# Expert groups of two and of three: another order within each layer

## The chip, the cores and the metric

The kernel runs on one core of a Trainium2 chip. The core has TensorE (PE in the profile) for matrix products, VectorE (DVE), ScalarE (ACT) and GpSimd (POOL) for the rest, and SyncE (SP), which here only issues transfers. Sixteen DMA engines carry the transfers of all queues. The metric is the device time of one execution in microseconds (us). [...]

## The reference, cut to what matters

The model is a trunk of two residual layers over 256 tokens of width 1024, all in float32, with a final norm. Each layer has attention, and then a mixture of sixteen experts, of which each token uses two:

```
aff = sigmoid(xf @ router_w)                  # 256 x 16
# the best of four groups of experts, in it the best two: expert (256 x 2), weight w (256 x 2)
for each expert e, for the tokens that chose it:
    h = silu(x @ w_gate[e]) * (x @ w_up[e])   # 1024 -> 512
    y = h @ w_down[e]                         # 512 -> 1024
x = x + gate_f * (sum over the two experts of w * y)
```

Each expert has three matrices of 2 MB, 6 MB in all; a layer's sixteen experts are 96 MB. Which expert gets how many tokens is known only when the router has run.

## The kernel before

The kernel never reads fewer than all experts. It sorts fourteen of the sixteen experts of a layer by their number of tokens (`places`, line 1357) and gives each a place with room for 96, 64 or 32 tokens: `GROUPS` (line 31) lists seven groups of places as (place, blocks of 32), each group 128 places wide, and `RANKS` (line 33) says which rank of the sorted experts goes to which place. The first group, places 14 and 15, is not sorted and holds the fixed experts 14 and 15, so its weights can be loaded before the router has run. Group 1 has two experts (96 and 32 places), groups 2 and 4 have three (64, 32, 32), groups 3, 5 and 6 have two (64 and 64). Tokens beyond an expert's room are done in overflow rounds.

A group's work (`Group`, line 1211) is: `hidden` loads gate and up and multiplies (16 steps over k, in each step one product per block of columns), `turn` transposes, `rows` loads down and multiplies (8 steps), and `late` adds the result to X. The loop at line 1464 runs `hidden` of group i, then `rows` of group i-1, then the gather of tokens for two later groups in every second turn.

Loads. Every matrix comes in two loads of 1 MB (`load_experts`, line 1161). They go into fifteen buffers of 1 MB, ten called slot and five called room. `left` (line 150) writes the cycle in which they are handed out: in layer 0 two rooms, five slots, three rooms, five slots; in layer 1 three rooms, six slots, two rooms, four slots. The cycle begins with four loads for the conditioning, then the eight of group 0's gate and up; the loads that need the router's result begin with the thirteenth. A load waits until its buffer has been given back by its last reader; of buffers of one kind the one given back first is taken first. SyncE issues nearly all loads, in the order of the program.

Line 1466 is the place that matters below. When the loop comes to group 3, the down of group 2 is loaded, the last sums are added, and `rest` (line 1445) reserves six buffers for overflow rounds and puts seven nested rounds behind a branch on their number. TensorE, ScalarE, VectorE and SyncE take this branch; with this input no round is needed. Group 3's own twelve loads are issued by GpSimd (`self.after`), which does not take the branch; SyncE goes on with group 4 behind it.

```
def left(n, then, more):
    order[:] = ["wx"] * n + ["w"] * then + ["wx"] * more + ["w"] * (RING - then)
...
def rest():
    space = [slot(4, 512) for _ in range(6)]
...
if i == 3:
    before.load_down()
    flush()
    rest()
```

In layer 1 the last group ends the kernel (`finish`, line 1283): its down comes in three pieces of 512, 256 and 256 columns (`load_down`, line 1251), and each is multiplied, weighted and added in turn, then the final norm is applied and stored.

Of the kernel before, what the change touches and what calls it, by code (L numbers as in the profile page):

```python
# [27 lines left out]
RING, EXTRA = 10, 5  # L28


GROUPS = [[(14, 2), (15, 2)], [(0, 3), (1, 1)], [(2, 2), (3, 1), (4, 1)], [(5, 2), (6, 2)], [(7, 2), (8, 1), (9, 1)],
          [(10, 2), (11, 2)], [(12, 2), (13, 2)]]
RANKS = 0, 9, 1, 10, 11, 2, 3, 4, 12, 13, 5, 6, 7, 8
SORTED = len(RANKS)
BLOCK = 32


def shape_constants():
# [40 lines left out]
    iota = np.tile(1000 + np.arange(96, dtype=f)[None], (P, 1))  # L79
    ranks = np.tile(np.array(RANKS, f)[None], (P, 1))  # L80
    places = sorted(x for g in GROUPS for x in g)
    size = np.tile(np.array([BLOCK * n for _, n in places], f)[None], (P, 1))

    owner = np.concatenate([np.repeat(np.eye(len(g), dtype=f), [BLOCK * n for _, n in g], axis=0) for g in GROUPS], axis=1)
    rank = np.tile((4 - np.arange(4)).astype(f)[None], (P, 1))
# [22 lines left out]
def trunk(ctx, tc, ins, out):  # L108
# [30 lines left out]
    def slot(n_k, n):  # L139

        tag = order.pop(0)
        order.append(tag)
        t = room() if tag == "wx" else ring.tile([P, 2048], F32, tag="w", name="slot")
        return t[:, :n_k * n].rearrange("p (k f) -> p k f", k=n_k)

    def room():

        return rooms.tile([P, 2048], F32, tag="wx", name="room")
# [818 lines left out]
    def moe(cp, wk, layer, norm, end):  # L967
# [119 lines left out]
        def blocks(group):  # L1087


            ns = [n for _, n in group]  # L1090
            if ns == [2, 2]:
                return [(1, slice(64, 128)), (0, slice(0, 64))]
            at = [a for a, n in enumerate(ns) for _ in range(n)]
            return [(at[j], slice(BLOCK * j, BLOCK * j + BLOCK)) for j in reversed(range(4))]
# [66 lines left out]
        def load_experts(nm, experts, k, tiles=None, queue=sp, fine=False):  # L1161

            out = [[] for _ in experts]
            for h in range(2):
                for i, e in enumerate(experts):
                    t = tiles.pop(0) if tiles else slot(4, 512)
                    v = ins[nm][layer][bass.ds(e, 1)].rearrange("o (p k) f -> p (o k) f", k=k)
                    n = k // 2
                    t = t.rearrange("p a b -> p (a b)").rearrange("p (k f) -> p k f", k=n)
                    if not (fine and h):  # L1170
                        queue.dma_start(t, v[:, n * h:n * h + n, :])
                    out[i].append((t, n))
            for k0 in range(0, n if fine else 0, 2):
                for x, e in zip(out, experts):
                    v = ins[nm][layer][bass.ds(e, 1)].rearrange("o (p k) f -> p (o k) f", k=k)
                    queue.dma_start(x[1][0][:, k0:k0 + 2, :], v[:, n + k0:n + k0 + 2, :])
            return [Rows(x) for x in out]
# [11 lines left out]
        def pick_tile():  # L1189
            return wk.tile([P, 2, 256], F32R, tag="pick", name="pick")  # L1190

        def picked(groups, pos):

            o = pick_tile()
            places, at = [x for g in groups for x in GROUPS[g]], 0
            while places:
# [14 lines left out]
        class Group:  # L1211


            def __init__(self, i, o, XG, c0):
                self.first, self.last = i == 0, (layer, i) == (1, len(GROUPS) - 1)
                self.after = i == 3
                self.o, self.XG, self.c0 = o, XG, c0
                self.p0, self.n = GROUPS[i][0][0], len(GROUPS[i])
                self.parts = blocks(GROUPS[i])
                first = sum(len(g) for g in GROUPS[:i])  # L1220
                self.owner = const("owner")[:, first:first + self.n]
                es = list(range(self.p0, self.p0 + self.n))
                if i:
                    es = [load_value(ex_p[:, e:e + 1], [(ET.SP, ET.Pool)[self.after]], NE - 1) for e in es]
                self.es = es
                self.Wd = None
# [24 lines left out]
            def load_down(self):  # L1251
                if self.Wd is not None:
                    return
                if not self.last:
                    self.Wd = load_experts("moe_w_down", self.es, 4, queue=(sp, pool)[self.after])
                    return

                src = [ins["moe_w_down"][layer][bass.ds(e, 1)].rearrange("o (p k) f -> p (o k) f", k=4) for e in self.es]
                self.Wd = []
                for sl, step in zip(end.pieces, (2, 4, 2)):  # L1260
                    n = sl.stop - sl.start
                    if n == 512:
                        tiles = [slot(4, n) for _ in range(2)]
                    else:
                        tile_ = slot(8, n)
                        tiles = [tile_[:, 0:4], tile_[:, 4:8]]
                    for k in range(0, 4, step):
                        for t, v in zip(tiles, src):
                            sp.dma_start(t[:, k:k + step], v[:, k:k + step, sl])
                    self.Wd.append(tiles)  # L1270
# [507 lines left out]
```

## Time and profile before

| | |
|---|---|
| median of 3 runs | 868.94 us (868.36 to 869.42) |
| the profiled execution's own time | 869.42 us |
| span of the profiled execution | 867.2 us |
| busy: TensorE, VectorE, ScalarE, GpSimd | 86%, 44%, 27%, 13% of the span |
| moved | 291.14 MB, a mean of 336 GB/s |
| the expert stage of layer 0 | from 232 to 464 us, 420 GB/s for most of it |
| the expert stage of layer 1 | from 618 us to the end |

The span runs from the first instruction to the last; the 2.2 us beside it belong to the execution and not to the trace. A row of a timeline names the engine, the line of the kernel, the tile that is written and the one that is read. The trace records each float32 product as two matrix instructions. Engine names that end in q are the engine's queue (its sequencer).

### The profile page before, as it was taken

The numbers are of one execution on the slowest core, as the hardware profiler recorded it, in microseconds if no ns is written. First come the engines' busy times: TensorE is split into PE (matmuls) and PEld (weight loads), VectorE is DVE, ScalarE is ACT, GpSimd is POOL, SyncE is SP. The second block draws the span as 40 slices with busy tenths as digits, with TensorE's granted clock in tenths as the row PEclk, the third lists the DMA queues.
The fourth block names the chain that finished last, engine by engine and source line by source line (L and its number), as shares of the span: only waits on it lengthen the run. The fifth ranks groups of instructions, "written<-read, shape, count | busy, mean of one in ns | idle before, by whom it ended". The sixth has DMA issues, their size and how long they took to land. (4 is left out here: it accounts for less than half of the span.)

```text
span 867.2 us, 12251 instructions
## 1 busy us (share of the span) xinstructions
PE 746.6 (86%) x4499; PEld 381.9 (44%) x4499; DVE 377.8 (44%) x1091; ACT 237.4 (27%) x569; POOL 115.6 (13%) x118
## 2 busy tenths in 40 slices
PE   4699999999799969759997899979899967769996
PEld 1298765557443332214332568556443322214233
DVE  2285777767831231103206654876912031103214
ACT  1254545545311010001112454545111010002012
POOL 2020111233100001000011223344000001000001
PEclk9699999999699999879999999988699988979998
DMA  9999878796299998999999997733499989999992
GB/s 328 349 328 387 321 248 217 280 376 219 96 422 418 419 417 337 419 420 419 419 415 389 360 350 196 288 130 122 179 419 419 419 361 395 420 420 419 416 396 77
DMA packets 84840, 291.14 MB, mean 336 GB/s; under 512 B 9174, under 2 KB 23202, under 8 KB 63010
## 3 DMA queue, kind: packets, MB, share of 16 engines
q1 hardware_dynamic: 76976, 258.36, 77.9%
q0 software_dynamic: 4608, 29.37, 8.3%
q10 hardware_dynamic: 3186, 2.51, 0.9%
q8 instruction: 39, 0.64, 0.3%
q14 instruction: 31, 0.25, 0.1%
HBM read 289.16 MB, written 1.06 MB: 335 GB/s over the span
## 5 line engine op out<-in xcount | busy, mean ns | idle before, releaser
L1084 PE MATMUL o<-slot,hT 128*32 128x512 f32 (+2 forms) x448 | 93.5, 619 | 14.0 <-PEq L1453 13.1
L1084 PE MATMUL sc<-slot,XG 128*64 128x512 f32 (+1 forms) x416 | 92.1, 646 | 13.6 <-DMA slot<-in_moe_w_up_dram 13.6
L1111 DVE TENSOR_TENSOR hq<-sc,hid 128x512 f32<-128x512 f32 x14 | 14.7, 1049 | 184.3 <-PE sc L1084 184.3
L1084 PE MATMUL mm<-slot,XG 128*32 128x512 f32 (+1 forms) x416 | 85.9, 624 | 5.2 <-DMA slot<-in_moe_w_gate_dram 5.2
L507 ACT CAST hl<-slot 128x512 fp32r<-128x512 f32 (+2 forms) x112 | 60.7, 557 | 72.8 <-PE mm L524 45.8
L464 POOL TENSOR_TENSOR hl<-slot,hl 128x512 fp32r<-128x512 f32 x40 | 53.2, 1333 | 163.1 <-ACT hl L507 135.7
L1084 PE MATMUL mm<-room,XG 128*64 128x512 f32 (+1 forms) x224 | 57.1, 629 | 5.6 <-DMA room<-in_moe_w_gate_dram 5.6
L1084 PE MATMUL o<-room,hT 128*32 128x512 f32 (+2 forms) x208 | 58.6, 603 | 2.0 <-DMA room<-in_moe_w_down_dram 2.0
L1155 DVE SCALAR_TENSOR_TENSOR adac<-o,w,GATE 128x512 f32<-128x512 f32 (+1 forms) x29 | 21.2, 732 | 82.5 <-PE o L1084 81.5
L522 PE MATMUL mm<-HH,hl 128*128 128x256 f32 x176 | 54.5, 311 | 2.3 <-ACT HH L496 2.3
L1084 PEld LDWEIGHTS sc<-slot,XG 128*64 128x64 f32 (+1 forms) x416 | 25.3, 132 | 70.1 <-issue 48.6
L1137 ACT CAST yg<-adac 128x512 fp32r<-128x512 f32 (+1 forms) x28 | 17.1, 612 | 140.0 <-DVE adac L1155 140.0
L332 PE MATMUL tp<-slot,csil 128*32 128x512 f32 x344 | 49.2, 648 | 4.4 <-DMA slot<-in_ada_w_dram 4.2
L1084 PE MATMUL sc<-room,XG 128*32 128x512 f32 (+1 forms) x224 | 45.0, 656 | 8.3 <-DMA room<-in_moe_w_up_dram 8.3
L1068 ACT ACTIVATE XG<-tp,mod,mod 128x256 f32<-128x256 f32 (+1 forms) x32 | 17.2, 538 | 124.0 <-PE tp L1066 124.0
L524 PE MATMUL mm<-HH,hl 128*128 128x256 f32 x176 | 50.0, 286 | 0.6 <-DVE hl L464 0.6
L523 PE MATMUL mm<-HH,hl 128*128 128x256 f32 x176 | 50.4, 287 | 0.1
L1084 PEld LDWEIGHTS o<-slot,hT 128*32 128x32 f32 (+1 forms) x448 | 25.5, 125 | 54.3 <-issue 36.0
L464 DVE TENSOR_TENSOR hl<-slot,hl 128x512 fp32r<-128x512 f32 (+2 forms) x72 | 42.6, 611 | 15.3 <-ACT hl L507 15.0
L1066 PE MATMUL tp<-pick,XH 128*128 128x256 f32 (+1 forms) x128 | 41.9, 347 | 4.0 <-DVE XG L1070 2.6
L1145 DVE TENSOR_TENSOR X<-X,tp 128x512 f32<-128x512 f32 (+1 forms) x56 | 36.0, 675 | 16.5 <-PE tp L1144 16.2
L1144 PE MATMUL tp<-yg,OT 128*128 128x512 f32 (+1 forms) x112 | 36.6, 431 | 7.5 <-ACT yg L1137 3.5
(377 smaller groups left out, 1305.9 us busy)
## 6 DMA issues: line engine op xcount, KB each, us to landing
slot<-in_ada_w_dram SPq DMA_DIRECT2D x43, 1024.0 KB, 10.3
slot<-in_moe_w_gate_dram SPq DMA_DIRECT2D x37, 1024.0 KB, 15.1
slot<-in_moe_w_down_dram SPq DMA_DIRECT2D x35, 1024.0 KB, 19.7
slot<-in_moe_w_up_dram SPq DMA_DIRECT2D x34, 1024.0 KB, 18.6
room<-in_moe_w_up_dram SPq DMA_DIRECT2D x20, 1024.0 KB, 16.8
room<-in_moe_w_gate_dram SPq DMA_DIRECT2D x19, 1024.0 KB, 15.2
room<-in_moe_w_down_dram SPq DMA_DIRECT2D x17, 1024.0 KB, 18.8
slot<-in_ev_w_in_dram SPq DMA_DIRECT2D x8, 1024.0 KB, 9.5
```

Source lines behind the costliest of these rows:

```text
L332: mm(b[g:g + 32], csil[:, k, 1 - half:33 - half], W[k], start=k < 4, stop=k >= 4)
L464: eng.tensor_tensor(lo, v, hi.bitcast(F32), ALU.subtract)
L507: act.copy(hi, src)
L522: mm(o, a[0], b[0], start=start, stop=False, skip_group_check=True)
L523: mm(o, a[0], b[1], start=False, stop=False, skip_group_check=True)
L524: mm(o, a[1], b[0], start=False, stop=stop, skip_group_check=True)
L1066: mm(b, xk[i][:, t, k, :], o[:, t, 0:n], start=t == i == 0, stop=t == i == 1)
L1068: act.activation(XG[:, k, :], b, AF.Identity, bias=sh[:, k:k + 1], scale=fa[:, k:k + 1])
L1084: last[0] = mm(*args, **kw)
L1144: mm(cb, OT[:, t, :], x, start=i == 0, stop=i == 1)
L1145: vec.tensor_tensor(X[:, t, sl], X[:, t, sl], cb, ALU.add)
L1155: vec.scalar_tensor_tensor(v, y, w, gate[:, sl], ALU.mult, ALU.mult)
```

## The change

`GROUPS` lists the same seven groups with the two groups of three experts at positions 5 and 6 instead of 2 and 4, and the places are numbered anew, so that a group's places still follow each other. `RANKS` is written for the new places; each rank keeps its number of blocks. Everything that goes by a group's position (GpSimd's loads for group 3, the reserved buffers before it, the pieces at the end of layer 1) now meets another group. Since the last group has three experts, `load_down` is written for any number of them: a piece of 512 columns takes one buffer for each expert, a piece of 256 columns one buffer for two, the third expert alone in a second one.

```diff
-GROUPS = [[(14, 2), (15, 2)], [(0, 3), (1, 1)], [(2, 2), (3, 1), (4, 1)], [(5, 2), (6, 2)], [(7, 2), (8, 1), (9, 1)],
-          [(10, 2), (11, 2)], [(12, 2), (13, 2)]]
-RANKS = 0, 9, 1, 10, 11, 2, 3, 4, 12, 13, 5, 6, 7, 8
+GROUPS = [[(14, 2), (15, 2)], [(0, 3), (1, 1)], [(2, 2), (3, 2)], [(4, 2), (5, 2)], [(6, 2), (7, 2)],
+          [(8, 2), (9, 1), (10, 1)], [(11, 2), (12, 1), (13, 1)]]
+RANKS = 0, 9, 1, 2, 3, 4, 5, 6, 7, 10, 11, 8, 12, 13
...
-                    if n == 512:
-                        tiles = [slot(4, n) for _ in range(2)]
-                    else:
-                        tile_ = slot(8, n)
-                        tiles = [tile_[:, 0:4], tile_[:, 4:8]]
+                    tiles = []
+                    while len(tiles) < len(src):
+                        tile_ = slot(2048 // n, n)
+                        tiles += [tile_[:, j:j + 4] for j in range(0, 2048 // n, 4)]
```

## Rows read from the trace of the kernel before

**Rows 1.** The chain that ended last, three pieces: start us, us, what.

```profile
740.55 30.74 DMA slot<-in_moe_w_up_dram
771.33 6.04 PE sc L1084 x32
...
855.92 1.90 PE o L1084 x16
```

**Rows 2.** Timeline of TensorE, last down of layer 0: start, us, what [idle before <-releaser].

```profile
464.34 0.64 PE L1084 MATMUL o<-room,hT 128*64 128x512 f32 x1 [1.08 <-DMA room<-in_moe_w_down_dram]
```

**Rows 3.** Windows, layer 0: length, busy by engine, TensorE clock, DMA share, GB/s.

```profile
230.00:235.00 5.00, 5.00 (x26) 5.00 (x25) 4.86 (x21) 1.37 (x3) 0.00 (x0) 0.50 0.41 116
...
325.00:330.00 5.00, 5.00 (x32) 1.30 (x35) 0.49 (x2) 0.00 (x0) 0.53 (x1) 0.59 0.32 131
330.00:335.00 5.00, 5.00 (x42) 1.55 (x36) 1.02 (x2) 0.62 (x1) 2.12 (x4) 1.00 0.93 341
```

**Rows 4.** Windows, layer 1: the branch and the end of the loads.

```profile
710.00:715.00 5.00, 4.78 (x24) 1.35 (x28) 0.76 (x2) 0.00 (x0) 0.00 (x0) 0.52 0.53 216
715.00:720.00 5.00, 5.00 (x44) 1.49 (x38) 0.75 (x1) 0.42 (x1) 2.65 (x5) 1.00 0.77 270
...
840.00:845.00 5.00, 4.31 (x22) 1.15 (x16) 1.39 (x2) 0.66 (x2) 0.00 (x0) 1.00 1.08 359
...
847.40:857.80 10.40, 10.40 (x59) 4.83 (x57) 6.03 (x10) 2.17 (x5) 1.16 (x1) 1.00 0.03 10
```

**Rows 5.** Line 1453, both layers: ns min/median/max, first and last start.

```profile
L1453 SPq EVENT_SEMAPHORE  x18: 17/17/17, 306.8 to 714.4; - x18
L1453 SPq COMPARE_BRANCH  x2: 50/50/50, 301.6 to 687.5; - x2
...
L1453 PEldq COMPARE_BRANCH  x2: 6131/6292/6452, 318.1 to 703.8; - x2
...
L1453 PEldq EVENT_SEMAPHORE  x2: 51/51/51, 324.6 to 710.0; - x2
```

**Rows 6.** Timeline of SyncE: first load after routing, loads around the branch.

```profile
231.94 1.91 SPq L1171 DMA_DIRECT2D slot<-in_moe_w_gate_dram  x3
...
300.85 0.33 SPq L1171 DMA_DIRECT2D room<-in_moe_w_down_dram  x1
329.38 0.33 SPq L1171 DMA_DIRECT2D room<-in_moe_w_gate_dram  x1
```

**Rows 7.** Waits of SyncE from 298 to 331 us: total, times, longest.

```profile
SPq L1453 <- SPq L1453: 27.0, 7, 5.3
```

**Rows 8.** Timeline of GpSimd, group 3's loads in layer 0, then layer 1.

```profile
304.70 0.63 POOL L1171 DMA_DIRECT2D room<-in_moe_w_gate_dram  x1 [83.70 <-DMA room<-in_moe_w_down_dram]
310.70 1.18 POOL L1171 DMA_DIRECT2D room<-in_moe_w_gate_dram  x2 [5.38 <-PE o L1084]
329.33 0.53 POOL L1171 DMA_DIRECT2D slot<-in_moe_w_gate_dram  x1 [17.45 <-SPq L1453]
...
715.09 0.53 POOL L1171 DMA_DIRECT2D room<-in_moe_w_gate_dram  x1 [17.14 <-SPq L1453]
```

**Rows 9.** Timeline of TensorE and VectorE, layer 0: products (start, us), last a pick.

```profile
244.78 3.60 PE L1084 MATMUL sc<-room,XG 128*64 128x512 f32 x16
248.22 3.60 PE L1084 MATMUL sc<-slot,XG 128*64 128x512 f32 x16
...
285.94 0.62 PE L1084 MATMUL mm<-slot,XG 128*32 128x512 f32 x2
...
296.27 3.62 PE L1084 MATMUL sc<-slot,XG 128*32 128x512 f32 x32
300.77 0.62 PE L1084 MATMUL o<-room,hT 128*32 128x512 f32 x1 [0.89 <-DMA room<-in_moe_w_down_dram]
...
306.78 3.64 PE L1084 MATMUL o<-room,hT 128*32 128x512 f32 x32
324.90 5.68 PE L1084 MATMUL o<-slot,hT 128*32 128x512 f32 x32 [6.84 <-PEq L1453]
...
324.73 0.76 DVE L1057 TENSOR_TENSOR pick<-K,placed 128x256 fp32r<-128x256 f32 x2 [5.95 <-PEq L1453]
```

## The prediction

> **What bounds the kernel now.** I read the chain of waits first, then the windows of DMA rate over the two expert stages, then the three queues around the branch that both stages contain. The chain shows two kinds of piece at its end: up to 771.3 us it runs through the landing of expert weights, and from there to the last instruction it stays on TensorE [rows 1]. So in layer 1 the weights set the pace until group 4, and TensorE sets the end. In layer 0 the last load of the stage is what TensorE waits for, by 1.08 us [rows 2]: there the transfer sets the end. The windows show that the transfers run at 420 GB/s through both stages, except at one place in each: at 325 to 335 us of layer 0 131 and 341 GB/s were moved [rows 3], at 710 to 720 us of layer 1 216 and 270 GB/s [rows 4]. Of each 5 us window the missing share of 420 GB/s is lost time: 3.44 + 0.94 = 4.4 us in layer 0, 2.43 + 1.79 = 4.2 us in layer 1. The layers repeat each other some 386 us apart [rows 5], so I work the branch out in layer 0 and carry it over.
>
> Why the hole is there: at the branch around the overflow rounds SyncE stays away from 301.6 us to its next load at 329.38 us [rows 5, 6], in seven steps of up to 5.3 us [rows 7]. GpSimd issues group 3 meanwhile, but gets only three loads out; the fourth waits for the branch [rows 8].
>
> **The change part by part.** The bytes are the same: 88 loads of 1 MB after routing in each layer, 2.50 us each at 420 GB/s. The capacity of each rank is the same too (rank 0 has 96 places, ranks 1 to 8 have 64, ranks 9 to 13 have 32), so the overflow rounds stay empty. TensorE's work stays: half of an eight-step product lasts 3.60 us with 64-column and 3.62 with 32-column blocks, 3.44 from start to start [rows 9]. The picks for the gathers become fewer early and more for groups 5 and 6 (four calls for one); VectorE is idle beside most of groups 3 to 6, so I take nothing; if that cover were gone it would be six comparisons, about 0.4 us each by the 0.76 us for two in the trace [rows 9], some 2.3 us.
>
> What moves is how much SyncE issues ahead of the branch. Before: 8 + 4 + 12 + 4 + 6 = 34 loads (groups 1 and 0, group 2 with three experts, the downs of 1 and 2). After: 8 + 4 + 8 + 4 + 4 = 28. Group 3's loads come behind, on GpSimd's queue, and each needs a buffer. With fifteen buffers in one cycle, the first load of group 3 goes where the load fifteen places earlier went. Before, counting back: six reserved by `rest`, six of group 2's down, so three of group 1's down remain; then come `rest`'s own. That is the three early issues of the trace [rows 8]. After: six of `rest`, four of group 2's down, so five remain: one of group 2's up and four of group 1's down, which TensorE has done with at 299.7 and 310.4 us (a little earlier without the 0.89 us wait at 300.77) [rows 9]. So 28 + 5 = 33 loads can be moved by the branch instead of 34 + 3 = 37.
>
> First stop, layer 0. The rate of the window 230 to 235 (116 GB/s, 1.38 us worth) puts the start of full rate at 233.6 us [rows 3]; 33 x 2.50 = 82.5 us later, at 316.1, nothing is left. SyncE comes to the branch once group 2's first gate half is used: group 2 starts at 285.94, 3.44 us on is 289.4, so it arrives near 290 and is back near 318 if its 27.7 us are fixed. But everything that is late next reuses `rest`'s buffers, which the rounds would have had TensorE read; I take it that such a buffer counts as free only when TensorE too has passed the branch. It arrives at 318.1 and leaves at 324.6 [rows 5]; 0.9 us earlier without that wait is 323.7. From an issue to flowing data the trace shows 329.38 to 330.94 and 715.09 to 716.79 (the ends of the partial windows), 1.6 to 1.7 us [rows 3, 4, 8]; with 0.15 us to the issue the flow returns at 325.45. The stop is 9.3 us, 4.9 more than the 4.4 lost now. No row of before shows the queues waiting for TensorE there: the other bound, SyncE as the last, is priced as a rival below, and the lower end is a loss of nothing at all.
>
> Second stop, layer 0 only. The cycle there has two rooms, five slots, three rooms, five slots; `rest` falls on five slots and one room. After the branch GpSimd can therefore issue two loads (a slot and the room), 5.0 us of transfer, to 330.45. The next two, GpSimd's last up and SyncE's first load of group 4, are rooms and wait for TensorE to finish a half product after the branch. The first such half took from 324.90 to about 330.6 us with a granted clock of 0.59 in that window, between the two levels (32 records in 5.68 us) [rows 3, 9], so it frees a room at 329.5 to 329.8 and the second 3.44 us later. Flow returns at 331.5 and 334.8: 1.1 + 0.8 = 1.9 us lost. Between 0 (both rooms free in time) and 8 us (another product is put first) I take 1.9, the order of the trace. In layer 1 the cycle is three rooms, six slots, two rooms, four slots: `rest` falls on two rooms and four slots, and the six loads that come next are of just these kinds. Six loads last 15 us; no second stop.
>
> From there to the end of layer 0 the transfers run at full rate in both versions, and TensorE has 20.6 us of products in a group (three of 6.88) and a few us of gathers and sums against 30 or 45 us of transfer, so nothing gives the delay back: layer 0 ends 4.9 + 1.9 = 6.8 us later. Attention follows from its last sum, and moves with it.
>
> Layer 1. The first stop is 8.8 us by the same sum (TensorE leaves at 710.0 - 0.9, flow returns at 710.9, the loads end at 702.1) against 4.2: 4.6 later. The last group has three experts: 1 MB more in 256-column pieces, at 359 instead of 420 GB/s [rows 4], 0.4 us. The loads end at 847.4 now (behind it the engines are 3% busy) and at 852.4 then. What this buys: now TensorE is still busy with two groups when the loads end, and its last product ends at 857.8 [rows 1, 4]. Afterwards the last two groups leave TensorE idle between loads, so the end hangs on the last load: 1.8 us from the end of flow to the signal (712.6 to 714.4 at the branch [rows 4, 5]), and half of the last 1.90 us product [rows 1]. That is 852.4 + 1.9 + 1.0 = 855.3, 2.5 us earlier than 857.8. The rest of the end is unchanged.
>
> Sum: +6.8 - 2.5 = +4.3 us on the profiled execution's 869.42 us, 873.7. That execution lies 0.48 us above the median of 868.94, so against the median it is 873.2; I predict 873.
>
> **The rivals.** *It gets faster, because SyncE's way through the branch is the last thing and it comes earlier.* Speaking for it: the trace names SyncE, not TensorE, as what GpSimd's fourth load waited for, 17.45 us [rows 8]. If SyncE's 27.7 us are fixed it is back at 318.0, flow at 319.6: the stop is 3.5 us. Layer 0 then has a second stop from 324.6 to 331.5, with the 0.8: 11.2 in all, +6.8; layer 1 gains 0.7, the end is 847.4 - 0.7 + 0.4 + 2.9 = 850.0, 7.8 earlier: -1.0 in all, 868. If instead the steps are a wait for outstanding loads to land, 28 loads are down by 306 and SyncE is back near 308: layer 1 has no stop, ends 11.3 earlier, and layer 0 stops once, from 321.1 to 331.5, with the 0.8 again +6.8: -4.5, 864. It decides where the releases of `rest`'s buffers do not include TensorE. Against it: the rounds have TensorE use them.
>
> [...]
>
> *No change.* The later end of layer 0 is given back whole. For it the end of layer 1 must gain 6.8 instead of 2.5: the signal of the last load and its product would have to be hidden, or the second stop be missing. 869 us.
>
> *Clearly slower.* After the branch TensorE takes group 3's gate before group 2's down, because its loads are in by then. One room is then free at 329.7 as above, but the second only after a whole gate and half a down, about 7 us later than I take it: +11, 880 us. For it speaks that group 3 stands first in the code; against it that now the down comes first [rows 9].
>
> **How the numbers follow.** Forecast 0.44, no change 0.20, clearly slower 0.17, faster 0.19 (of it 0.06 at the price of 868, which counts as no change with some of its width, and the rest towards 864). The forecast's own range is 871 to 876. Leaving out a tenth on either side, 866 to 880 holds the case of no change, most of the clearly slower one and half of the faster one. Within 0.2% (1.7 us, about what a measurement of this kernel can tell from no change) I give 0.22, faster 0.17, slower 0.61.
>
> **What would show it.** Right: three early loads on GpSimd's queue become five; the flow stops near 316 us and returns with TensorE's end of the branch, not with SyncE's; a short second stop near 331 in layer 0 and none in layer 1; at the end of layer 1 TensorE waits for the last loads. Wrong: SyncE's absence ends the stop, or the rate does not fall to nothing before 318 us, or TensorE still runs without a wait after the loads end.

## The result, and the profile after

The kernel after takes 874.75 us (median of 5 runs, 872.52 to 876.54), the kernel before on the same chip 868.36 us (866.21 to 869.42). The ratio is 1.0078, 95% interval 1.006 to 1.0095: slower by 6.4 us. The profiled executions are 872.52 and 869.42 us long (spans 870.8 and 867.2), the shortest of the one kernel and the longest of the other, so the traces have only 3.6 us of the 6.4 to show.

| milestone, us | before | after | later by | forecast |
|---|---|---|---|---|
| layer 0: the last load is there, its half product starts | 464.34 | 470.51 | 6.2 | 6.8 |
| layer 0: last sum starts on TensorE | 470.97 | 479.70 | 8.7 | 6.8 |
| layer 1: first load after routing | 617.98 | 622.49 | 4.5 | 6.8 |
| layer 1: the loads stop flowing | 847.4 | 855.4 | 8.0 | 11.8 |
| layer 1: first product behind the last down | 858.38 | 862.10 | 3.7 | 4.3 |

The windows of the kernel after over the branch in layer 0 answer to [rows 3] (length, busy time by engine, TensorE clock, DMA share, GB/s):

```profile
305.00:310.00 5.00, 3.71 (x33) 1.69 (x28) 0.54 (x1) 1.13 (x2) 1.06 (x2) 1.00 0.71 246
310.00:315.00 5.00, 4.45 (x38) 2.04 (x28) 3.06 (x5) 2.04 (x4) 1.06 (x2) 1.00 0.81 293
315.00:320.00 5.00, 3.73 (x15) 1.80 (x13) 3.36 (x6) 0.71 (x2) 0.00 (x0) 1.00 0.95 388
320.00:325.00 5.00, 1.86 (x6) 0.71 (x8) 1.17 (x8) 0.00 (x0) 1.05 (x2) 0.70 0.19 31
325.00:330.00 5.00, 5.00 (x18) 1.65 (x16) 0.00 (x0) 0.00 (x0) 0.11 (x1) 0.62 0.92 374
330.00:335.00 5.00, 5.00 (x28) 1.97 (x25) 2.47 (x6) 1.51 (x3) 0.42 (x1) 1.00 0.85 277
335.00:340.00 5.00, 5.00 (x26) 1.72 (x24) 0.40 (x1) 0.00 (x0) 0.53 (x1) 1.00 0.98 410
```

Against 420 GB/s the first five lose 2.07 + 1.51 + 0.38 + 4.63 + 0.55 = 9.1 us, the last two 1.70 + 0.12 = 1.8 us. So there are two stops, of the sizes forecast (9.3 and 1.9); but the first is no clean one, the rate sags from 305 us on and is near nothing only in the window from 320 us. GpSimd's timeline (start, us, what [idle before <-releaser]) says why, and answers to [rows 8]:

```profile
299.08 0.63 POOL L1171 DMA_DIRECT2D room<-in_moe_w_gate_dram  x1 [78.43 <-PE sc L1084]
306.21 1.21 POOL L1171 DMA_DIRECT2D slot<-in_moe_w_gate_dram  x2 [6.50 <-PE o L1084]
312.87 0.53 POOL L1171 DMA_DIRECT2D slot<-in_moe_w_gate_dram  x1 [5.45 <-PE o L1084]
313.52 0.53 POOL L1171 DMA_DIRECT2D slot<-in_moe_w_up_dram  x1
323.23 0.53 POOL L1171 DMA_DIRECT2D slot<-in_moe_w_up_dram  x1 [9.18 <-PEq L1452]
324.00 0.53 POOL L1171 DMA_DIRECT2D room<-in_moe_w_up_dram  x1 [0.24 <-issue]
329.89 0.53 POOL L1171 DMA_DIRECT2D room<-in_moe_w_up_dram  x1 [5.36 <-PE o L1084]
```

Five early issues instead of three; the sixth waits for TensorE's end of the branch, the eighth is a room that waits for a half product. Between 306.2 and 312.9 us all of SyncE's loads ahead of the branch have been moved and GpSimd has no free buffer: its second buffer and the three behind it came free with group 1's down, whose halves TensorE ran later than the prediction had them (done by 305.9 and 312.5 us, not 299.7 and 310.4):

```profile
302.29 3.64 PE L1084 MATMUL o<-slot,hT 128*32 128x512 f32 x32
308.95 3.64 PE L1084 MATMUL o<-slot,hT 128*32 128x512 f32 x32
```

Two rows of SyncE's waits (total, times, longest), the first from 285 to 335 us, the second from 676 to 714 us, say that SyncE itself is through early in both layers and then waits for TensorE:

```profile
SPq L1171 <- PE o L1084: 24.3, 1, 24.3
...
SPq L1171 <- PEq L1452: 12.1, 1, 12.1
```

Layer 1, against [rows 4]: one stop of 1.42 + 1.45 + 0.30 + 3.81 = 7.0 us (4.2 before), at full rate right behind it; the last row shows the loads ending at 855.4 us.

```profile
695.00:700.00 5.00, 3.71 (x33) 1.73 (x29) 0.54 (x1) 1.13 (x2) 1.06 (x2) 1.00 0.83 301
700.00:705.00 5.00, 4.46 (x39) 2.01 (x29) 3.02 (x5) 2.01 (x4) 1.06 (x2) 1.00 0.81 298
705.00:710.00 5.00, 3.77 (x15) 1.84 (x13) 3.40 (x6) 0.75 (x2) 0.00 (x0) 1.00 0.95 395
710.00:715.00 5.00, 2.54 (x6) 0.86 (x8) 1.17 (x8) 0.00 (x0) 1.58 (x3) 0.61 0.37 100
715.00:720.00 5.00, 5.00 (x20) 1.76 (x18) 0.00 (x0) 0.00 (x0) 0.00 (x0) 0.70 1.01 423
...
855.00:860.00 5.00, 4.62 (x66) 2.42 (x68) 2.86 (x6) 1.77 (x6) 2.53 (x2) 1.00 0.12 37
```

TensorE's rows of the branch, both layers (ns min/median/max, first and last start), answer to [rows 5]. It arrives at 318.9 and 708.7 us and needs 3.9 and 3.5 us for the branch, which took 6.5 and 6.1 before:

```profile
L1452 PEldq COMPARE_BRANCH  x2: 3471/3695/3919, 318.9 to 708.7; - x2
...
L1452 PEldq EVENT_SEMAPHORE  x2: 51/51/51, 322.9 to 712.2; - x2
```

At the end of layer 0, where before had one wait of 1.08 us [rows 2], TensorE idles 5.39 us ahead of the last load's half product. The window behind it has a granted clock of 0.50; before, the same half ran at 1.00. These are the two readings of most 1 us windows: 1.00 in 748 and 0.50 in 92 of 870 in the trace of the kernel after, 735 and 104 of 867 before. First the timeline of the kernel after, then the window:

```profile
470.51 1.06 PE L1084 MATMUL o<-room,hT 128*32 128x512 f32 x1 [5.39 <-DMA room<-in_moe_w_down_dram]
477.39 1.50 PE L1144 MATMUL tp<-yg,OT 128*128 128x512 f32 x4 [0.73 <-ACT yg L1137]
479.70 1.23 PE L1144 MATMUL tp<-yg,OT 128*128 128x512 f32 x4 [0.80 <-DVE X L1145]
```

```profile
470.50:474.00 3.50, 3.49 (x20) 0.87 (x24) 0.00 (x0) 0.00 (x0) 2.00 (x8) 0.50 1.04 386
```

From that product's start to the first sum 470.51 to 477.39 = 6.9 us go by; before it was 464.34 to 468.69 = 4.4. So 2.5 us were added there.

The chain of waits (start us, us, what) answers to [rows 1]. It stays on the landing of weights up to 839.87 us instead of 771.33, and from there runs through TensorE and the sums:

```profile
822.32 17.51 DMA room<-in_moe_w_down_dram
839.87 2.83 PE o L1084 x24
...
850.60 1.90 PE o L1084 x16
852.52 0.76 DVE adac L1155
853.37 0.63 ACT yg L1137
854.03 0.72 PE tp L1144 x2
...
855.49 1.91 PE o L1084 x32
857.42 0.49 DVE adac L1155
```

The load that ends the DMA part is group 5's down, not the last one. Behind the end of the loads (855.4 us) TensorE's waits are short, and none is for a load:

```profile
858.45 1.14 PE L1144 MATMUL tp<-yg,OT 128*128 128x256 f32 x4 [0.24 <-ACT yg L1137]
...
862.10 0.70 PE L1526 MATMUL mm<-adac,OT 128*128 128x256 f32 x2 [1.50 <-DVE adac L1155]
```

### The profile page after: what moved, and what is told of

It is laid out like the page before. It is cut to its first block, busy times and chain, and to the rows that moved or that the text cites. A ratio compares the mean times of both kernels' runs of the same rounds, so it can differ in the third digit from the quotient of the medians.

```text
span 870.8 us, 12292 instructions
## 1 busy us (share of the span) xinstructions
PE 747.6 (86%) x4515; PEld 383.5 (44%) x4515; DVE 379.1 (44%) x1095; ACT 236.9 (27%) x569; POOL 112.6 (13%) x118
## 5 line engine op out<-in xcount | busy, mean ns | idle before, releaser
L1084 PE MATMUL o<-slot,hT 128*32 128x512 f32 (+2 forms) x496 | 101.4, 654 | 10.1 <-DMA slot<-in_moe_w_down_dram 6.5
L1084 PE MATMUL mm<-slot,XG 128*32 128x512 f32 (+1 forms) x432 | 93.9, 627 | 2.4 <-DMA slot<-in_moe_w_gate_dram 2.4
L1084 PE MATMUL sc<-slot,XG 128*32 128x512 f32 (+1 forms) x360 | 70.4, 598 | 9.0 <-DMA slot<-in_moe_w_up_dram 9.0
L1084 PE MATMUL sc<-room,XG 128*32 128x512 f32 (+1 forms) x280 | 56.2, 614 | 7.4 <-DMA room<-in_moe_w_up_dram 7.4
L1084 PE MATMUL mm<-room,XG 128*32 128x512 f32 (+1 forms) x208 | 57.7, 655 | 0.0
L1084 PE MATMUL o<-room,hT 128*32 128x512 f32 (+2 forms) x176 | 45.6, 632 | 13.1 <-DMA room<-in_moe_w_down_dram 8.8
L1084 PEld LDWEIGHTS o<-slot,hT 128*32 128x32 f32 (+1 forms) x496 | 28.0, 132 | 57.8 <-issue 50.1
L1084 PEld LDWEIGHTS sc<-slot,XG 128*32 128x32 f32 (+1 forms) x360 | 19.6, 121 | 50.9 <-issue 38.2
L1084 PEld LDWEIGHTS mm<-slot,XG 128*32 128x32 f32 (+1 forms) x432 | 23.0, 126 | 42.1 <-issue 36.8
```

The lines of the kernel that those rows point to most:

```text
L1084: last[0] = mm(*args, **kw)
```

## The experiments

**Which of the two places, the branch or the end of a layer.** Only the order of the groups differs; `RANKS` goes with it, so that each rank keeps its capacity.

```
# three at 2 and 6
GROUPS = [[(14, 2), (15, 2)], [(0, 3), (1, 1)], [(2, 2), (3, 1), (4, 1)], [(5, 2), (6, 2)], [(7, 2), (8, 2)],
          [(9, 2), (10, 2)], [(11, 2), (12, 1), (13, 1)]]
# three at 4 and 5
GROUPS = [[(14, 2), (15, 2)], [(0, 3), (1, 1)], [(2, 2), (3, 2)], [(4, 2), (5, 2)], [(6, 2), (7, 1), (8, 1)],
          [(9, 2), (10, 1), (11, 1)], [(12, 2), (13, 2)]]
```

> The groups with three experts stand second and last (before: 2 and 4; after: 5 and 6): up to the branch this is the kernel before, at the end of the layers the kernel after. Theory A (the loss lies at the branch, in the loads that can be moved ahead of it): GpSimd has three early issues as before, the rate falls for 4.4 us only; the last group costs the end of layer 0 some 2.6 us (TensorE idles ahead of the last weights and runs its last product at the lower clock) and gains some 4 us at the end of layer 1: 865 to 868 us. Theory B (the loss lies in the last group of a layer, which now ends on its own weights): the whole +6.4 us is here, 874 to 875 us.

> The groups with three experts stand at 4 and 5, the last group has two: up to the branch this is the kernel after, at the end of the layers the kernel before. Theory A (branch): five early issues, the rate falls by 6 us more in layer 0 and 2.6 us more in layer 1 than in the kernel before, and nothing is gained at the end: 874 to 878 us. Theory B (last group): 868 to 870 us.

Measured: 865.8 us for 2 and 6, ratio to the kernel before 0.9977 (0.9964 to 0.9991), so 2.0 us faster; 875.48 us for 4 and 5, ratio 1.0086 (1.0067 to 1.0105), so 7.5 us slower. With the branch's half of the change alone the loss is whole, with the end's half alone there is a small gain: theory A. The traces say the same layer by layer. With 4 and 5 layer 0's last sum starts 4.8 us later than in the kernel before, and layer 1 (from its first load to the first product behind the last down) is 0.7 us longer; with 2 and 6 the two numbers are 2.2 us later and 3.0 us shorter. The attention stage between them, in which the edit changes nothing, differs as well: 147.13 us with 4 and 5, 142.67 with 2 and 6, 147.01 in the kernel before (the last section has more on that), so the gain of 2 and 6 is only in part one of the expert stages. The windows at the branch follow suit. Three at 2 and 6 has the single fall of the kernel before, in this window; three at 4 and 5 has the long one of after:

```profile
325.00:330.00 5.00, 5.00 (x32) 1.27 (x31) 0.57 (x4) 0.00 (x0) 0.73 (x2) 0.59 0.33 133
```

```profile
315.00:320.00 5.00, 2.92 (x10) 1.19 (x8) 2.79 (x5) 0.56 (x1) 0.00 (x0) 1.00 0.82 346
320.00:325.00 5.00, 3.12 (x8) 1.12 (x10) 1.04 (x6) 0.00 (x0) 1.06 (x2) 0.53 0.37 88
```

Three at 2 and 6 beats both kernels.

**Without the branch.** In both kernels the call of `rest` goes, and with it the branch, the rounds and their six buffers; the two runs do not tell the branch from the buffers.

```
             if i == 3:
                 before.load_down()
                 flush()
-                rest()
```

> The kernel after without the branch and without the overflow rounds behind it (left out of the computation; they are empty with this input), and without the six buffers reserved for them. Theory A: the rate doesn't fall between 300 and 340 us nor near 710; all loads end 8.9 us earlier in layer 0 and some 7 us in layer 1, of which the clock at the end of layer 0 and TensorE's own work at the end of layer 1 may keep a part: 860 to 864 us. Theory B: only the few us of the branch instructions themselves go, 870 to 873 us.

> The kernel before without the branch and the overflow rounds (left out, empty with this input). Theory A: the two falls of the rate, 4.4 and 4.2 us, go, and layer 1 ends on TensorE's backlog: 860 to 865 us, and the difference to the kernel after without the branch is within 3 us instead of 6.4. Theory B: the difference to the other kernel without the branch stays 6 us or more.

Measured: 856.07 us in the order of after (ratio to the kernel before 0.9851, 0.9827 to 0.9875) and 864.32 us in the order of before (0.9955, 0.9939 to 0.9971). The branch costs the new order some 19 us and the old one 4. Without it the new order is the faster one by 8 us, more than either theory said: theory B is out, and A had the size too small (860 to 864 us for the order of after, and a difference within 3 us). In the traces 9.9 us of the new order's gain lie in layer 0 and 5.8 in layer 1, and its attention stage is 3.5 us longer than in the kernel after. The rate of the order of after no longer falls below 411 GB/s between 235 and 440 us; this is the window that stood at 31:

```profile
320.00:325.00 5.00, 5.00 (x22) 1.85 (x24) 2.13 (x4) 0.00 (x0) 0.00 (x0) 1.00 1.02 419
```

The order of before gained less than its two stops because it gets new ones: 351 and 339 GB/s at 345 to 355 us, where GpSimd's next load waits 40.4 us for an up product to free its buffer, and 297 and 300 GB/s at 725 to 735 us. They lose 1.8 and 2.9 us of the 8.6 that the old stops cost.

**More loads ahead of the branch than either kernel has.**

```
# three at 1 and 6
GROUPS = [[(14, 2), (15, 2)], [(0, 2), (1, 1), (2, 1)], [(3, 2), (4, 2)], [(5, 3), (6, 1)], [(7, 2), (8, 2)],
          [(9, 2), (10, 2)], [(11, 2), (12, 1), (13, 1)]]
# three at 1 and 2
GROUPS = [[(14, 2), (15, 2)], [(0, 2), (1, 1), (2, 1)], [(3, 2), (4, 1), (5, 1)], [(6, 3), (7, 1)], [(8, 2), (9, 2)],
          [(10, 2), (11, 2)], [(12, 2), (13, 2)]]
```

> The groups with three experts stand first behind the unsorted one and last (1 and 6). Ahead of the branch SyncE issues 12 + 4 + 8 + 6 + 4 = 34 loads, and group 2's down has four, so five issues of GpSimd come early: 39 loads can be moved by the branch (37 in the kernel before, 33 in the one after). Theory A (the stop is the time by which these loads end before the flow returns): 39 x 2.50 = 97.5 us behind 233.6, the flow would end at 331; TensorE leaves the branch near 325 as before, the flow returns near 326 to 327: no stop but a thinner stretch while GpSimd's early issues wait for TensorE, 0 to 2 us lost in place of 4.4 and 4.2, and the end as with three at 2 and 6: 858 to 863 us. Theory C (the stop follows group 2's own size, as its up product sets when TensorE comes to the branch): a stop as in the kernel after, and 871 to 874 us.

> The groups with three experts stand first, at 1 and 2: 12 + 4 + 12 + 6 + 6 = 40 loads of SyncE ahead of the branch and three early issues of GpSimd, 43 in all. Theory A: the flow could last to 341 us; TensorE gets group 2's last up load near 306 us (295 in the kernel before) and leaves the branch near 333, the flow returns before it has ended: nothing lost in either layer, and an end like that of the kernel before, where TensorE is behind: 860 to 865 us. Theory C: TensorE's later arrival at the branch moves the stop along with it, 867 to 870 us.

Measured: 865.08 us for 1 and 6, ratio 0.9959 (0.9939 to 0.998), 3.5 us faster than before; 868.47 us for 1 and 2, ratio 1.0002 (0.9981 to 1.0023). Both miss the times of theory A. Theory C misses at 1 and 6 (871 to 874 us); at 1 and 2 the time is in its range, but the stop from which it came is not there. At 1 and 6 the count was right (five early issues) and the arrival wrong: TensorE comes to the branch at 328.4 us, not 318, so GpSimd's third early load goes out only at 324.27 us, and 292, 323, 316 and 331 GB/s in the four windows from 320 us lose 5.0 us. From 230 to 440 us 84.5 MB are moved, 84.7 in the kernel before: nothing is gained at the branch, so what it gains lies behind it. In its trace layer 0's last sum starts 2.4 us later (473.35), layer 1 is 1.1 us shorter, and the attention stage 3.5 us shorter (143.51). At 1 and 2 the stop is gone as A said, and the time is not. These are its windows at the branch (TensorE leaves it at 340.2 us) and late in layer 1:

```profile
335.00:340.00 5.00, 0.00 (x0) 0.00 (x0) 0.00 (x0) 0.00 (x0) 0.00 (x0) 0.78 1.01 411
340.00:345.00 5.00, 4.52 (x24) 1.29 (x28) 0.76 (x2) 0.00 (x0) 2.11 (x4) 0.54 0.95 349
760.00:830.00 70.00, 68.48 (x355) 26.31 (x355) 17.96 (x32) 10.28 (x18) 0.00 (x0) 1.00 1.01 418
```

Only 0.85 us is lost. But TensorE is then busy 68.5 of 70 us from 760 to 830 us (60.75 in the kernel before): with the long groups in front its own work moves to the back, and the saved transfer time ends as TensorE's backlog. In layer 0 it is the same: TensorE is busy 118.2 of the 130 us from 340 to 470 us (107.0 in the kernel before), and the last sum starts at 471.42, no earlier. That the backlog keeps the saved time is read from these rows, not tested by itself.

**The second stop.** One line of the kernel after, the order of the fifteen buffers in layer 0:

```
-        left(2, 5, 3)
+        left(3, 6, 2)
```

> The kernel after with layer 1's cycle of the fifteen buffers (three rooms, six slots, two rooms, four slots) in layer 0 too, so that the six buffers reserved there are four slots and two rooms. If the second stop of layer 0 (277 GB/s at 330 to 335 us) comes from the kind of buffer that GpSimd's last up and SyncE's first load of group 4 need, it goes: layer 0 ends some 2 us earlier, 872 to 873 us. If it comes from the queue alone (few loads in flight behind a standstill), it stays: 874 to 875 us.

Measured: 871.81 us, ratio to before 1.0046 (1.003 to 1.0062), against 1.0078 of the kernel after: 2.8 us less, just below the 872 to 873 us expected. Windows from 320 us:

```profile
320.00:325.00 5.00, 3.35 (x8) 1.11 (x10) 1.17 (x8) 0.00 (x0) 1.58 (x3) 0.50 0.52 156
325.00:330.00 5.00, 5.00 (x22) 1.76 (x20) 0.00 (x0) 0.00 (x0) 0.00 (x0) 0.82 1.02 431
330.00:335.00 5.00, 5.00 (x28) 1.95 (x26) 2.87 (x6) 1.51 (x3) 0.00 (x0) 1.00 1.01 418
```

Nothing is lost behind 325 us: the kinds of buffer made the second stop. SyncE also returns at 321.48 us instead of 333.06, since its first load no longer needs a buffer that a half product frees, which shortens the first stop too (156 GB/s for 31 from 320 to 325 us).

**The low clock at the end of layer 0.** The kernel after with ten, then five, products added:

```
                 for k in range(4):
+                    if k == 2 and (layer, self.p0) == (0, GROUPS[-1][0][0]):
+                        b = bank("sc", [P, 512])
+                        for _ in range(5):
+                            put(b, ident, self.hT.rearrange("p k m -> p (k m)"), start=True, stop=True)
```

> The kernel after with ten products more (identity by the hidden values, into a bank that nothing reads) on TensorE ahead of the second half of layer 0's last product, where it idles 5.4 us and then works at a granted clock of 0.50. If the idle time is what lowers the clock there, the half product behind the last load takes 3.6 us instead of 5.6 and layer 0's last sum comes some 2 us earlier: 872 to 873 us. If the clock falls for another reason, the half stays at 5.6 us and the time at 874 to 876 us.

> The kernel after with five products more, instead of ten, ahead of the second half of layer 0's last product (ten lasted past the landing of the last weights). If TensorE's idle time is what lowers the clock there: granted clock 1.00 behind the last load, the half product in 3.5 us instead of 5.6, 872 to 873 us. If the clock has no part in the time: 874 to 876 us.

Measured: 876.53 us with ten (ratio 1.0095, 1.0066 to 1.0123), 876.04 us with five (1.0087, 1.0073 to 1.0101). Ten kept TensorE busy at a clock of 1.00 until 473.66 us, beyond the landing. With five, the timeline at the last product (the load's landing, then layer 0's last sum) and its window are:

```profile
470.62 0.62 PE L1084 MATMUL o<-room,hT 128*32 128x512 f32 x1 [1.17 <-DMA room<-in_moe_w_down_dram]
...
477.28 1.25 PE L1144 MATMUL tp<-yg,OT 128*128 128x512 f32 x4 [0.79 <-DVE X L1145]
```

```profile
470.00:474.00 4.00, 3.38 (x32) 0.94 (x32) 0.53 (x1) 0.00 (x0) 2.02 (x8) 1.00 1.04 387
```

The load lands at the same time (470.62, 470.51), the clock stays at 1.00 and the last sum comes 2.4 us earlier. So it is the idle time that lowers the clock here (0.50 behind 5.39 us of it, 1.00 behind 1.17), and that costs 2.4 us at this place. The time of the whole kernel did not follow: both runs lie above the 874 to 876 us that were to show that the clock has no part. The attention behind it took 148.6 us here and 142.8 in the kernel after; the last section has more on that.

**The branch two groups later.** In each order, twice in the code:

```
-                self.after = i == 3
+                self.after = i == 5
...
-            if i == 3:
+            if i == 5:
```

> The order of the kernel after, with the branch two groups later, ahead of group 5 instead of group 3, and group 5's loads on GpSimd's queue instead of group 3's. Theory A (the stop is what the loads ahead of the branch leave uncovered of TensorE's way to it, and at group 3 TensorE is still behind its loads): 52 loads of SyncE and five early ones of GpSimd, 57 x 2.50 = 142.5 us behind 233.6, flow to 376; TensorE, no longer behind, comes to the branch near 370 and leaves it near 375: a stop of 0 to 2 us, and most of what the kernel without the branch gained comes back: 858 to 864 us. Theory D (a branch costs its stop wherever it stands, because SyncE's loads drain and TensorE's pass takes the same): 872 to 876 us.

> The order of the kernel before, with the branch ahead of group 5 and group 5's loads on GpSimd's queue. Theory A: the falls of 4.4 and 4.2 us go, as in the kernel before without the branch (864.3): 862 to 866 us, slower than the order of after with the branch at 5, because that order ends better. Theory D: 867 to 870 us.

Measured: 880.91 us in the order of after (ratio to before 1.017, 1.0139 to 1.0202), 879.89 us in the order of before (1.013, 1.0114 to 1.0146). Both worse than either theory. My assumption that TensorE is no longer behind at group 5 was wrong: in the order of after it comes to the branch at 380.5 us, not 370, and the five windows from 365 to 390 us lose 10.2 us:

```profile
365.00:370.00 5.00, 3.71 (x18) 1.39 (x14) 0.54 (x1) 0.56 (x1) 1.06 (x2) 1.00 0.41 110
370.00:375.00 5.00, 4.89 (x24) 2.02 (x24) 1.45 (x3) 1.31 (x3) 0.49 (x1) 1.00 0.93 387
375.00:380.00 5.00, 4.48 (x19) 2.78 (x20) 3.79 (x8) 2.00 (x4) 0.57 (x2) 1.00 0.85 305
380.00:385.00 5.00, 0.73 (x4) 0.24 (x5) 1.16 (x2) 0.00 (x0) 0.20 (x1) 1.00 0.30 121
385.00:390.00 5.00, 5.00 (x18) 1.85 (x16) 0.00 (x0) 0.00 (x0) 2.44 (x5) 0.66 0.91 321
```

In the order of before the transfers lose 5.3 us, about as at group 3, and yet layer 0's last sum comes 5.5 us later (476.51). That the weights of two groups then share the queues and leave TensorE their work for the end is my reading, not a tested one.

**A second profile of the kernel after.**

> The kernel after once more, unchanged, for a second profiled execution. In the first one the attention stage between the layers (from layer 0's last sum to layer 1's first load) took 142.8 us at a granted clock of 0.95; in the kernel before 147.0 us at 0.92, with the same 726 products. Theory E (the clock granted there differs from one execution to the next, whatever the order of the groups): the stage can be anywhere from 142.5 to 148.5 us and follows its clock; the median is again 873 to 876 us. Theory F (the later end of layer 0 makes the stage 4 us shorter, so the attention gives part of the delay back): 142.8 us within 0.5 again.

Measured: 875.11 us (ratio 1.0084, 1.0066 to 1.0102); the stage again took 142.7 us at a clock of 0.95. Both theories allow that, so this run does not settle between them. The two profiled executions are also the shortest of their series, with the highest granted clocks in them (0.938 and 0.939 over the whole core; 0.928 to 0.939 in the others), so they say little of the longer ones. The reason that theory F gives, a later end of layer 0, does not fit the other traces: the order of before without the branch starts layer 0's last sum at 468.79 us and has the short stage too (142.75), and the order of before with the branch at 5 starts it at 476.51 and has a long one (148.42).

## Why the prediction was right, step by step

**The prediction's own signs.** Five early issues, a flow that returns with TensorE's end of the branch, and a second stop in layer 0 alone came as said. Two of the three signs of being wrong came too: at 315 to 320 us the rate was still 388 GB/s, so it did not fall to nothing before 318 us, and behind the end of the loads TensorE no longer waits for one. The first changed the shape of a term and not its size; the second is the term that failed, below.

**33 loads for 37, five early issues for three.** As forecast, to the issue. That this count of what runs ahead of the branch is the loss is shown by three at 4 and 5, which has nothing of the change's ending, and by the kernels without the branch. The count alone does not set the size: at 1 and 6, with 39 loads, 5.0 us were lost, since TensorE came 10 us later than I had it.

**First stop, layer 0: 9.3 forecast, 9.1 measured,** through two errors that cancel. TensorE arrived at 318.9 us instead of 317.2, since the down products ran between gathers, at 302.29 and 308.95 us; and its branch took 3.9 us instead of 6.5. The shape (nothing from 316 us on) was wrong. The sum depends only on how many loads are moved by the time of TensorE's exit, and that it came out to 0.2 us is luck: the arrival was 1.7 us late and the branch 2.6 us short.

**What ends the stop.** TensorE's exit, in both layers: it leaves the branch at 322.9 and 712.2 us, and the next loads are issued at 323.23 (GpSimd) and 712.28 us (SyncE). The rival that SyncE is last is out: it waits 12.1 us for TensorE in layer 1. Nor does a run show its way through the branch as fixed at 27.7 us, on which the price of 868 us for that rival rested: in layer 1 it lasts from 678.4 to 699.5, 21.1 us.

**Second stop: 1.9 forecast, 1.8 measured,** and gone with other kinds of buffer. TensorE took group 2's down first, as before (GpSimd's last up waits for a product into `o`, the output of a down), so the rival at 880 us is out.

**The end of layer 0: 6.8 forecast.** The last load is 6.2 us later, but the last sum 8.7: the forecast let the layer end move with its loads, and left out that TensorE, idle for 5.4 us, runs the last product at the lower clock (0.50).

**First stop, layer 1: 4.6 forecast, 2.8 measured.** The branch of 3.5 us instead of 6.2 is the mis-sized term, less TensorE's arrival, 1.3 us later against the start of the layer than I had it.

**The end: -2.5 forecast for layer 1 as a whole, -0.8 measured** (3.7 - 4.5). The step that failed is "the end hangs on the last load". The last loads come with pieces of the output whose sums form a chain of their own (product, scaling, split, sum, one behind the other, as from 850.60 to 854.75 us in the chain of waits), and this chain had begun with group 5's down at 839.87 us. From the end of flow to the first product behind the last down 6.7 us go by; with 2.9 us to the end of the last down's product I had counted about 3.5. With the branch of before the same end does better: three at 2 and 6 gains 3.0 us in layer 1 (853.23 - 858.38 against first loads 615.79 - 617.98).

**The sum.** 6.2 + 2.5 - 4.2 - 0.8 = +3.7 us in the two traces, forecast +4.3. The -4.2 us belong to the attention stage, for which I had nothing; without them the layers lose 7.9 us, 3.6 more than forecast. So the mechanism at the branch was right, and that the sum of the traces is so near the forecast is luck: the low clock in layer 0 (+2.5) and the smaller gain at the end (1.7 less) are made up for by an attention stage that happened to be shorter. The medians differ by 6.4 us and the profiled executions' own times by 3.1; the 3.3 us between lie in executions without a trace, so where they are lost is open. The rival of no change needed 6.8 us back at the end; what came back there was 0.8.

## What to carry to other kernels

Ahead of a branch that several queues pass, count the loads that can be out before the last engine leaves it, and work out when that engine comes: what wasn't issued then was lost bandwidth here (9.1 us in layer 0 with 33 loads, 4.4 with 37), and what stands behind the branch gave back 0.8 us of it. A large batch ahead of the branch raised the count (39 loads at 1 and 6), but it also made the engine come later (328.4 us, 318.1 in the kernel before). The gain of the new ending had to be read from the chain behind the last-but-one batch (from 839.87 us on), not from the last load alone: 0.8 us instead of 2.5. And taking a stop away did not shorten the time where TensorE set the end: with both large groups in front 0.85 us were lost, but TensorE was busy 68.5 of the 70 us from 760 us on, and the time stayed at 868.47 us. And a forecast that meets the time is checked term by term: here two terms that nobody had forecast, +2.5 and -4.2 us, stand behind the agreement.

## What the hardware showed unexpectedly

**TensorE's branch is longer where more is moved beside it.** Over the twelve profiles of kernels with the branch, two passes each, it lasts 3.4 to 4.2 us where the transfers move 96 to 138 GB/s meanwhile (14 passes) and 5.9 to 6.6 us where they move 379 to 412 GB/s (10 passes); none lies between. Which of the two sets the other is not shown: the short passes are all in orders in which the queues ran dry at the branch. The rows give the lengths and name no cause.

**The attention stage's length varies with the same work.** From layer 0's last sum to layer 1's first load it took 142.7 to 148.6 us in the fourteen profiles, with nearly the same number of products in each (728 or 729 records), and it goes with the granted clock: 142.7 to 144.5 us at 0.95 or 0.96, 145.4 to 148.6 at 0.91 to 0.94. The rows of the stage, kernel before and kernel after (one window each):

```profile
472.00:618.00 146.00, 129.48 (x725) 88.57 (x724) 99.59 (x310) 68.63 (x183) 47.89 (x33) 0.92 0.66 228
```

```profile
481.00:622.40 141.40, 125.58 (x724) 86.36 (x724) 100.41 (x310) 68.68 (x184) 45.97 (x33) 0.95 0.66 227
```

TensorE's busy time is 3.9 us shorter in the second, with nearly the same records (725 and 724). Two profiles of the kernel after agree within 0.1 us. What decides in which stretch the clock falls was not found; the spread of 5.9 us is enough to hide or to double a change of a few us upstream, as in the kernel with five products more.
